# Turning the second half's input rows by VectorE ahead of time, by way of DRAM, instead of by TensorE amid the projections

## The chip, the cores and the metric

One core of a Trainium2 chip runs the whole step. The metric is device time in microseconds. Before the change the median of three runs is 1445.81 us (1445.39 to 1446.68).

## The reference

One layer of a hybrid decoder: prompt of 2048 tokens (`x_prompt`, 1024 wide) and 8 sample tokens, everything in float32.

```
ada = silu(c) @ w_ada + b_ada
shift, scale, gate = split(ada, 3)
hn = rmsnorm(x, g_norm) * (1 + scale) + shift
z = hn @ w_in                                    # 1024 -> 5136 columns
xa, za, q, k, v, glr, zg = split(z)
# LRU group: conv4 over xa, two block-diagonal gates, linear recurrence, times silu(za)
# GLA group: 4 heads, o = chunked linear attention of q, k, v with decay from glr,
#            o = rmsnorm(o) * g_gla_norm, times silu(zg)
x = x + gate * (concat(y_lru, y_gla) @ w_out)
y = rmsnorm(x, g_final)
```

The rows of `x` lie with tokens first; a projection on TensorE wants `hn` with its 1024 features on the partitions. So each block of 128 tokens has to be normalised, turned (128 tokens x 1024 features become 8 blocks of 128 features x 128 tokens), and modulated by scale and shift, which after the turn are values per partition (`Gm`, `Sh`).

## The kernel before, in words

The prompt is worked in two halves of 1024 tokens. The turned `hn` of the current half stays in SBUF as two tiles, `hh` (rounded to the matmul's type) and `hl` (what the rounding left), and a product of `hn` with a weight is three matmuls: high with high, low with high, high with low (L661 to L663 in `project`, L346 to L348 for values). Weights of `w_in` are split the same way by ScalarE and VectorE in the first half, stored to DRAM as `parts`, and loaded from there in the second (L293, `w<-parts`, 1 MB for a pair of high and low).

The program is written by a driver with a clock of its own (`tick`, `after`): `after(units, fn)` puts a piece of work in a heap, and it is written out when the clock has passed that time. A second list, `drips`, holds pieces that `project` writes out between its matmuls, one for every two steps of the contraction (every four for 256 columns). A scheduler then orders the instructions of each engine by its own model of time, so an engine's order is fixed when the program is built; each engine works its order through, and an instruction that waits holds up what stands behind it. `behind(V)` has it put an instruction directly after the last one on VectorE. SP's queue issues most of the DMAs, and is in order too.

Tiles come from pools with a fixed number of buffers: `xt` (tag "xt" in pool `xp`) has two, PSUM `acc` four, PSUM `tp` two. Whoever takes a buffer again waits until it was read.

The place of the change is the end of half 0, `lru_last_a`, in which the last LRU column tile (`xa_unit`, `za_unit`, gates L1315 to L1317) is projected for half 0 while `hh` and `hl` are overwritten, 256 tokens at a time, by the second half's:

- `hn_load(g)` for g = 0 to 3 loads two blocks of 128 rows of the second half (L256; into the two `xt` buffers for g = 0, into three `xst` tiles for g = 1 to 3), and `normalize` squares and sums them (ScalarE, L165), takes 1/sqrt by twelve small VectorE steps (L147 to L153) and scales (L181).
- `next_hn` calls `modulate`, dripped: eight transposes by TensorE for four of the eight feature blocks of a pair of row blocks (L197, into `tp`), an eviction with scale and bias by ScalarE (L199, L201; for g = 3 every second one by VectorE, L203), the high part by GpSimd (L204) and the low part by VectorE (L205).

After it comes `gates_ahead`: the gate columns of one head over the new half, as two products of 256 tokens, two more of 256 and two of 512 (evicted by L1129 and L1130, stored to `zgd`), the sums of quarter blocks of `hn` that a seven-product scheme needs (`sums`, L1491 to L1500 on VectorE, `drips` as well), and the products themselves (`seven`, L1559).

Of the kernel before, what the change touches and what calls it, by code (L numbers as in the profile page):

```python
# [8 lines left out]
F32 = mybir.dt.float32  # L9
F32R = mybir.dt.float32r  # L10
I32 = mybir.dt.int32
AF = mybir.ActivationFunctionType
OP = mybir.AluOpType

P = 128
D = 1024
KT = D // P
T = 2048
TH = T // 2
NS = 8  # L20
# [34 lines left out]
def hybrid_kernel(ctx, tc, i, o):  # L55
    nc = tc.nc
    V, S, G, PE, SP = nc.vector, nc.scalar, nc.gpsimd, nc.tensor, nc.sync

    const = ctx.enter_context(tc.tile_pool(name="const", bufs=1))
    dpool = ctx.enter_context(tc.tile_pool(name="dpool", bufs=1, space=bass.MemoryType.DRAM))  # L60
    psum = ctx.enter_context(tc.tile_pool(name="psum", bufs=1, space=bass.MemoryType.PSUM))

    def acc():
        return psum.tile([P, 512], F32, tag="acc", name="acc", bufs=4)

    def tps():
        return psum.tile([P, 512], F32, tag="tp", name="tp", bufs=2)
# [7 lines left out]
    wd2 = dpool.tile([2, P, 2, 4, 512], F32, tag="wd2", name="wd2")  # L75
    zd = dpool.tile([16, P, D], F32, tag="zd", name="zd")
    zgd = dpool.tile([8, P, TH + NS], F32, tag="zgd", name="zgd")
    a21d = dpool.tile([2, P, 4, 512], F32, tag="a21d", name="a21d")
    twd = dpool.tile([3 + len(EARLY), 4, P, 2, 512], F32, tag="twd", name="twd")

    ident = const.tile([P, P], F32, name="ident")
# [4 lines left out]
    xp = p1.enter_context(tc.tile_pool(name="xp", bufs=2))  # L86
# [24 lines left out]
    Gm = cp.tile([P, KT, 9], F32, name="Gm")  # L111
    Sh = cp.tile([P, KT, 9], F32, name="Sh")
# [29 lines left out]
    def rsqrt(pool, out, ss, n, rows, scale):  # L142

        y = pool.tile([P, 16], F32, tag="rs_y", name="rs_y", bufs=1)[:rows, :n]
        t = pool.tile([P, 16], F32, tag="rs_t", name="rs_t", bufs=1)[:rows, :n]
        x = pool.tile([P, 16], F32, tag="rs_x", name="rs_x", bufs=1)[:rows, :n]
        V.tensor_scalar(x, ss, scale, EPS, op0=OP.mult, op1=OP.add)  # L147
        V.tensor_scalar(t.bitcast(I32), x.bitcast(I32), 1, None, op0=OP.logical_shift_right)
        V.tensor_scalar(y.bitcast(I32), t.bitcast(I32), -1, 0x5F3759DF, op0=OP.mult, op1=OP.add)
        for it in range(3):  # L150
            V.tensor_tensor(t, y, y, op=OP.mult)
            V.scalar_tensor_tensor(t, t, -0.5, x, op0=OP.mult, op1=OP.mult)
            V.scalar_tensor_tensor(out if it == 2 else y, t, 1.5, y, op0=OP.add, op1=OP.mult)  # L153
# [9 lines left out]
    def square_sum(pool, out, x, m, n, tag="f512"):  # L163
        junk = pool.tile([P, 1024], mybir.dt.bfloat16, tag=tag, name="junk", bufs=2)
        S.activation(junk[:m, :n], x, AF.Square, accum_out=out)  # L165

    def squares(pool, xt, m=P, tag="f512", ss=None, j0=0):
        if ss is None:
            ss = pool.tile([P, 4], F32, tag="ss", name="ss", bufs=2)
        for j, x in enumerate(xt, j0):  # L170
            square_sum(pool, ss[:m, j:j + 1], x[:m], m, D, tag)
        return ss

    def scales(pool, ss, n, m=P):
        rs = pool.tile([P, 4], F32, tag="rs", name="rs", bufs=2)
        rsqrt(pool, rs[:m, :n], ss[:m, :n], n, m, 1.0 / D)
        return rs

    def times(xt, rs, m=P, j0=0):
        for j, x in enumerate(xt, j0):  # L180
            V.tensor_scalar(x[:m], x[:m], rs[:m, j:j + 1], None, op0=OP.mult)  # L181

    def normalize(pool, xt, m=P, tag="f512"):

        times(xt, scales(pool, squares(pool, xt, m, tag), len(xt), m), m)

    def modulate(xt, g, kts):

        c = slice(g * 256, (g + 1) * 256)
        for k2 in range(kts[0], kts[1], 2):  # L190
            pt = tps().rearrange("p (k t) -> p k t", k=2)
            cg = slice(g % 2 * 256, g % 2 * 256 + 256)
            f = (fs4[(1, 2, 0)[k2 // 4 if g < 2 else 2]][:, k2 % 4:k2 % 4 + 2, cg] if g < 2 or k2 >= 4
                 else ra[k2 // 2][:, :, cg])
            for kt in range(2):
                for j in range(2):
                    PE.transpose(pt[:, kt, j * P:(j + 1) * P],  # L197
                                 xt[j][:, (k2 + kt) * P:(k2 + kt + 1) * P], ident)
            S.activation(f[:, 0], pt[:, 0], AF.Identity, scale=Gm[:, k2, 8:9], bias=Sh[:, k2, 8:9])  # L199
            if g < 3:  # L200
                S.activation(f[:, 1], pt[:, 1], AF.Identity, scale=Gm[:, k2 + 1, 8:9], bias=Sh[:, k2 + 1, 8:9])  # L201
            else:
                V.tensor_scalar(f[:, 1], pt[:, 1], Gm[:, k2 + 1, 8:9], Sh[:, k2 + 1, 8:9], op0=OP.mult, op1=OP.add)  # L203
            G.tensor_scalar(hh[:, k2:k2 + 2, c], f, 1.0, 0.0, op0=OP.mult, op1=OP.add)  # L204
            V.tensor_tensor(hl[:, k2:k2 + 2, c], f, hh[:, k2:k2 + 2, c].bitcast(F32), op=OP.subtract)  # L205

# [35 lines left out]
            V.tensor_tensor(hl[:, kt, :256], f[:, j], hh[:, kt, :256].bitcast(F32), op=OP.subtract)  # L242
        split(1)

    def hn_load(g, now=True):

        xt = []
        for j in range(2):
            q = 2 * g + j
            if q < 2:  # L250
                x = xp.tile([P, TH + NS], F32, tag="xt", name="xt")[:, :D]
            else:
                n = q - 2
                x = xst[n // 2][:, n % 2]
            t0 = TH + q * P
            SP.dma_start(x, i["x_prompt"][0, t0:t0 + P])  # L256
            xt.append(x)
        if now:
            normalize(xp, xt)
        return xt  # L260

    fs = cp.tile([P, KT, NS], F32, name="fs")
# [174 lines left out]
    with tc.tile_pool(name="ada", bufs=1, side="right") as ap:  # L437
# [79 lines left out]
        with in_order():  # L517
# [13 lines left out]
            pt = turn(xt0[0:2], (0, 1))  # L531
# [10 lines left out]
            for c in range(1, 4):  # L542
                k = (2 * c, 2 * c + 1)
                if c > 1:
                    ada(c, (0, KT))
                pt = [turn(xt0, (kt,)) for kt in k]
# [134 lines left out]
    def behind(q):  # L681

        return tc.issue_after(next(x for x in reversed(list(nc.cur_bb.bb.instructions)) if x.engine == q.engine))
# [17 lines left out]
    def after(units, fn, gla=False, val=False):  # L701
        clock[1] += 1
        heapq.heappush(pend, (clock[0] + units, clock[1], fn, gla, val))
# [17 lines left out]
    def ada_gate():  # L721

        pg = acc()

        def step(kt):
            ws = [xp.tile([P, TH + NS], F32, tag="xt", name="xt")[:, :D] for _ in range(2)]
            for n, w in enumerate(ws):
                SP.dma_start(w, i["w_ada"][0, (kt + n) * P:(kt + n + 1) * P, 2 * D:])

            def mm():  # L730
                for n in (1, 0):
                    for g in range(4):
                        PE.matmul(pg[32 * g:32 * g + 32, :256], sc[:, kt + n], ws[n][:, g * 256:(g + 1) * 256],
                                  start=kt == 0 and n == 1, stop=kt == KT - 2 and n == 0)
                if kt + 2 < KT:
                    step(kt + 2)
                else:
                    gr = xp.tile([P, 512], F32, tag="f512", name="gr")[:, :256]
                    S.copy(gr, pg[:, :256])
                    SP.dma_start(gated, gr)  # L740
                    after(4, lambda: ready("gate"))
            after(3, mm)

        step(0)


    so, fs4, xst, ra, waiting = {}, [], [], [], ["gate", "pairs"]
    outw = {"stop": False, "next": None, "busy": False}

    def ready(what):  # L750
        nonlocal hp
        waiting.remove(what)
        if what == "pairs":
            hpx.close()
            hp = hpx.enter_context(tc.tile_pool(name="hp", bufs=1, reuse_waits="tile"))
        if not waiting:
            out_weights()
# [670 lines left out]
    def next_hn(xt, g, k):  # L1428

        modulate(xt[g], g, (k, k + 4))  # L1430
        if (g, k) == (1, 0):
            normalize(xp, xt[3])

    def lru_last_a(js):

        xa_load, xa_unit, za_load, za_unit = lru_units(0)
        xt = [hn_load(0)]
        lru(0, js[:-2])
        outw["stop"] = True
        lru(0, js[-2:-1])  # L1440
        t = xa_load(js[-1])
        za_load(t)
        flush_gla()
        while outw["busy"]:
            heapq.heappop(pend)[2]()
        open_sp()
        xt += [hn_load(1), hn_load(2), hn_load(3, False)]
        for s in range(2):
            xa_unit(t, s)
            za_unit(t, s)  # L1450
            for g in range(2 * s, 2 * s + 2):
                for k in range(0, KT, 4):
                    drips.extend([lambda g=g, k=k: next_hn(xt, g, k), lambda: None])
# [503 lines left out]
    for x in pairs[:2]:  # L1957
        x.new(A11)
        r = wp.tile([P, 1088], F32, tag="wr", name="wr")[:, :D].rearrange("p (q k t) -> p q k t", q=2, k=4)
# [215 lines left out]
    for n in range(2, 16):  # L2175
        g = n - 1
        x, prev = pairs[n], pairs[n - 1]
# [16 lines left out]
    for q in range(8):  # L2194
        g, k = 2 + q // 2, q % 2
# [63 lines left out]
```

## Time and profile before

| what | before |
|---|---|
| median of 3 runs | 1445.81 us |
| the profiled execution | 1445.69 us |
| its span | 1443.8 us, so 1.9 us lie outside the span |
| mean granted TensorE clock | 0.998 |
| busy share PE, DVE, ACT, POOL | 98%, 73%, 48%, 15% |
| HBM | 188.51 MB read, 115.33 MB written, 210 GB/s over the span |
| TensorE transposes of L197 | 64, from 558.7 to 588.0 us |

PE is TensorE, DVE VectorE, ACT ScalarE, POOL GpSimd, SP SyncE; PEld are TensorE's weight loads, and a q behind an engine's name its queue. A row of a timeline has the start, the duration, the engine, the line, the operation, what it writes and reads, and in brackets the idle time before it with what ended it. A row of groups has the count, the busy time, the mean of one in ns, and the idle time before it. Half 0's projections fill about 80 to 560 us, the turn of the second half's rows 547 to 590, the products of the second half follow from there.

### The profile page before, as it was taken

Reading aid. Unit: us, or ns where it says so; the run is one execution under the profiler, and the core shown is the slowest. Engines: PE = TensorE matmul, PEld = TensorE weight load, DVE = VectorE, ACT = ScalarE, POOL = GpSimd, SP = SyncE. Lnnn points to the kernel's source line nnn. Section 1 sums busy time; section 2 is a strip of 40 time slices with the busy share of each in tenths; the row PEclk is TensorE's granted clock in tenths of the full one; section 3 lists DMA queues with packets and bytes.
Section 4 is the critical chain, followed back from the end, with each engine's and each line's share of the span. In section 5 each row is a group of like instructions: output and inputs, shape, how many; then the busy total and the mean of one; then the engine's idle time right before and its main releaser. Section 6 shows DMA issues by size and latency. Waiting matters only on the chain.

```text
span 1443.8 us, 23568 instructions
## 1 busy us (share of the span) xinstructions
PE 1421.8 (98%) x8741; PEld 1250.8 (87%) x8741; DVE 1050.4 (73%) x2473; ACT 689.4 (48%) x1251; POOL 220.5 (15%) x366
## 2 busy tenths in 40 slices
PE   8999999999999999999999999999999999999998
PEld 6889979899898988878899999999998887778886
DVE  5767658776676678955458688686888986688886
ACT  3654444663445358624354454635557622144342
POOL 0200112122112013100111422334210000000000
PEclk9999999999999999999999999999999999999999
DMA  9755785874565546577744665665671767694453
GB/s 321 278 186 176 251 274 191 259 244 148 192 218 189 182 162 228 177 245 236 286 148 151 210 237 178 225 198 182 238 254 66 293 231 267 227 353 144 134 166 117
DMA packets 160856, 305.33 MB, mean 211 GB/s; under 512 B 12962, under 2 KB 90434, under 8 KB 158301
## 3 DMA queue, kind: packets, MB, share of 16 engines
q1 hardware_dynamic: 106837, 217.39, 44.1%
q0 software_dynamic: 22912, 70.96, 14.4%
q10 hardware_dynamic: 30992, 15.47, 3.6%
q8 instruction: 69, 1.13, 0.3%
q14 instruction: 46, 0.38, 0.1%
HBM read 188.51 MB, written 115.33 MB: 210 GB/s over the span
## 4 chain that ended last, share of the span: by engine, by line
PE 79%; DVE 9%; ACT 4%; issue 3%; DMA 3%; SPq 1%; POOL 0%; ACTq 0%; DVEq 0%; POOLq 0%
PE acc L1845 12%; PE acc L661 11%; PE acc L663 11%; PE acc L662 11%; PE tp L1845 9%; PE acc L1559 6%; PE acc L346 3%; PE acc L347 3%; PE acc L348 3%; PE po L1072 2%; PE acc L1315 1%; PE tp L1163 1%; PE acc L1317 1%; PE acc L1316 1%; PE tp L1041 1%
## 5 line engine op out<-in xcount | busy, mean ns | idle before, releaser
L661 PE MATMUL acc<-hh,w 128*128 128x512 f32 (+3 forms) x1112 | 377.4, 339 | 0.3 <-ACT tx L1318 0.2
L663 PE MATMUL acc<-hh,w 128*128 128x512 f32 (+3 forms) x1112 | 375.1, 337 | 0.0
L662 PE MATMUL acc<-hl,w 128*128 128x512 f32 (+3 forms) x1112 | 375.0, 337 | 0.0
L661 PEld LDWEIGHTS acc<-hh,w 128*128 128x128 f32 x1112 | 209.3, 188 | 16.8 <-ACT tx L1318 0.9
L663 PEld LDWEIGHTS acc<-hh,w 128*128 128x128 f32 x1112 | 209.2, 188 | 16.1
L662 PEld LDWEIGHTS acc<-hl,w 128*128 128x128 f32 x1112 | 209.3, 188 | 15.1
L1845 PE MATMUL acc<-w,a 128*128 128x512 f32 (+1 forms) x792 | 184.9, 387 | 0.0
L1845 PEld LDWEIGHTS acc<-w,a 128*128 128x128 f32 x792 | 146.8, 188 | 33.2 <-issue 3.4
L346 PE MATMUL acc<-w,hh 128*128 128x256 f32 (+1 forms) x508 | 143.9, 283 | 0.0
L348 PE MATMUL acc<-w,hl 128*128 128x256 f32 (+1 forms) x508 | 142.8, 281 | 0.1
L347 PE MATMUL acc<-w,hh 128*128 128x256 f32 (+1 forms) x508 | 142.7, 281 | 0.0
L1845 PE MATMUL tp<-w,a 128*128 128x512 f32 x564 | 136.1, 391 | 0.0
L1845 PEld LDWEIGHTS tp<-w,a 128*128 128x128 f32 x564 | 105.2, 188 | 26.9 <-issue 5.2
L346 PEld LDWEIGHTS acc<-w,hh 128*128 128x128 f32 x508 | 95.6, 188 | 1.3 <-ACT zs L1129 0.4
L348 PEld LDWEIGHTS acc<-w,hl 128*128 128x128 f32 x508 | 96.1, 189 | 0.3 <-DVE hl L228 0.3
L347 PEld LDWEIGHTS acc<-w,hh 128*128 128x128 f32 x508 | 95.5, 188 | 0.2
L1129 ACT ACTIVATE zs<-acc 128x512 f32<-128x512 f32 (+3 forms) x70 | 34.4, 492 | 107.8 <-PE acc L663 102.8
L1695 ACT CAST a<-s 128x512 fp32r<-128x512 f32 x61 | 36.5, 620 | 95.0 <-issue 35.5
L1278 DVE SCALAR_TENSOR_TENSOR cv<-xa,vecT,cv 128x512 f32<-128x512 f32 (+2 forms) x120 | 76.6, 641 | 3.1 <-ACT cv L1276 2.7
L1130 DVE SCALAR_TENSOR_TENSOR zs<-zs,acc 128x512 f32<-128x512 f32 (+3 forms) x70 | 38.4, 548 | 46.8 <-ACT zs L1129 46.8
L956 ACT CAST vh<-acc 128x256 fp32r<-128x256 f32 x56 | 20.4, 370 | 86.2 <-PE acc L348 70.8
L957 DVE TENSOR_TENSOR vl<-acc,vh 128x256 fp32r<-128x256 f32 x56 | 23.2, 419 | 47.6 <-ACT vh L956 47.6
(409 smaller groups left out, 2757.5 us busy)
## 6 DMA issues: line engine op xcount, KB each, us to landing
parts<-w SPq DMA_DIRECT2D x37, 1024.0 KB
w<-parts SPq DMA_DIRECT2D x28, 1024.0 KB
wr<-in_w_in_dram SPq DMA_DIRECT2D x38, 512.0 KB
a<-mixd SPq DMA_DIRECT2D x63, 256.0 KB
w<-wd SPq DMA_DIRECT2D x12, 1024.0 KB
w<-twd SPq DMA_DIRECT2D x20, 512.0 KB
wada<-in_w_ada_dram SPq DMA_DIRECT2D x16, 512.0 KB
mixd<-zs ACTq DMA_DIRECT2D x32, 256.0 KB
```

The lines of the kernel that those rows point to most:

```text
L346: PE.matmul(ps, hh[:, kt, c], hi[:, kt % 4], start=kt == 0, stop=False)
L347: PE.matmul(ps, hh[:, kt, c], lo[:, kt % 4], start=False, stop=False)
L348: PE.matmul(ps, hl[:, kt, c], hi[:, kt % 4], start=False, stop=kt == KT - 1)
L661: PE.matmul(ps[:, :n], hi[:, kt], a, start=kt == 0, stop=False)
L662: PE.matmul(ps[:, :n], hi[:, kt], b, start=False, stop=False)
L663: PE.matmul(ps[:, :n], lo[:, kt], a, start=False, stop=kt == KT - 1)
L1129: S.activation(z, ps, AF.Tanh, scale=0.5)
L1130: V.scalar_tensor_tensor(z, z, 1.0, ps, op0=OP.add, op1=OP.mult)
L1278: V.scalar_tensor_tensor(cv[:, cq], xa[:, cq.start + k:cq.stop + k], cw[k], cv[:, cq], op0=OP.mult, op1=OP.add)
L1559: PE.matmul(ps, w[:, u, k], x[v][k], start=start and (k, u, v) == (0, 0, 0), stop=(k, u) == (3, 1), skip_group_check=True)
L1695: S.copy(t[:, 0, k], (low(t) if src is None else src)[:, k])
L1845: PE.matmul(ps, t[:, u, k], w[:, v, k, c], start=(q < 3 or ps is own) and (k, u, v) == (0, 0, 0), stop=(k, u) == (3, 1), skip_group_check= ...
```

## The change

The second half's eight blocks of rows are no longer turned by TensorE. From the end of `ada_gate` on, early in half 0, a chain written by `after` handles one block q after another: load the rows (an `xt` buffer), three clock units later square and sum them, then the small steps and the scaling, then a VectorE transpose of all 32x32 blocks of the 128x1024 tile into the other `xt` buffer, then a store to a new DRAM tile `xtd[q]`, then the next block. VectorE turns each 32x32 block in place within its group of 32 partitions. What is left of the turn, the exchange of partition groups and column groups, is done by the addresses of the loads: `hn_load` reads `xtd` with four DMAs for each tile, one for each group of 32 partitions, in pieces of 1 KB (twenty loads where there were eight). `modulate` then reads the turned tiles in SBUF: no PSUM, and for g = 0 twice as many, half as wide ScalarE instructions, since the two blocks lie in two tiles.

```diff
+    xtd = dpool.tile([8, P, D], F32, tag="xtd", name="xtd")
...
     def modulate(xt, g, kts):
...
+        pt = [x.rearrange("p (n k t) -> p k n t", k=KT, t=32) for x in xt]
         for k2 in range(kts[0], kts[1], 2):
-            pt = tps().rearrange("p (k t) -> p k t", k=2)
...
-            for kt in range(2):
-                for j in range(2):
-                    PE.transpose(pt[:, kt, j * P:(j + 1) * P],
-                                 xt[j][:, (k2 + kt) * P:(k2 + kt + 1) * P], ident)
-            S.activation(f[:, 0], pt[:, 0], AF.Identity, scale=Gm[:, k2, 8:9], bias=Sh[:, k2, 8:9])
-            if g < 3:
-                S.activation(f[:, 1], pt[:, 1], AF.Identity, scale=Gm[:, k2 + 1, 8:9], bias=Sh[:, k2 + 1, 8:9])
-            else:
-                V.tensor_scalar(f[:, 1], pt[:, 1], Gm[:, k2 + 1, 8:9], Sh[:, k2 + 1, 8:9], op0=OP.mult, op1=OP.add)
+            for kt in range(k2, k2 + 2):
+                for j, y in enumerate(pt):
+                    n = 256 // len(pt)
+                    z = f[:, kt - k2, j * n:(j + 1) * n].rearrange("p (n t) -> p n t", t=32)
+                    if g < 3 or kt == k2:
+                        S.activation(z, y[:, kt], AF.Identity, scale=Gm[:, kt, 8:9], bias=Sh[:, kt, 8:9])
+                    else:
+                        V.tensor_scalar(z, y[:, kt], Gm[:, kt, 8:9], Sh[:, kt, 8:9], op0=OP.mult, op1=OP.add)
             G.tensor_scalar(hh[:, k2:k2 + 2, c], f, 1.0, 0.0, op0=OP.mult, op1=OP.add)
...
+    def turn_ahead(q):
+
+        x, w = [xp.tile([P, TH + NS], F32, tag="xt", name="xt")[:, :D] for _ in range(2)]
+        SP.dma_start(x, i["x_prompt"][0, TH + q * P:TH + (q + 1) * P])
+
+        def scaled(ss):
+            with behind(V):
+                times([x], scales(xp, ss, 1))
+            after(0.5, turned)
+
+        def turned():
+            with behind(V):
+                V.transpose(w.rearrange("p (c k j) -> p c k j", c=4, k=KT), x.rearrange("p (k c j) -> p c k j", c=4, k=KT))
+            after(0.5, stored)
+
+        def stored():
+            SP.dma_start(xtd[q], w)
+            if q < 7:
+                after(1, lambda: turn_ahead(q + 1))
+
+        def squared():
+            ss = squares(xp, [x])
+            after(0.5, lambda: scaled(ss))
+
+        after(3, squared)
+
+    def hn_load(g):
+
+        if g == 0:
+            xt = [xp.tile([P, TH + NS], F32, tag="xt", name="xt")[:, :D] for _ in range(2)]
+        else:
+            xt = [xst[g - 1].rearrange("p q d -> p (q d)")]
+        m = 2 // len(xt)
+        for j, x in enumerate(xt):
+            src = xtd[2 * g + j * m:2 * g + j * m + m].rearrange("q (a r) (c f) -> c r (q a) f", a=4, c=4)
+            for c in range(4):
+                SP.dma_start(x[32 * c:32 * c + 32].rearrange("r (n f) -> r n f", f=256), src[c])
         return xt
...
     def next_hn(xt, g, k):
 
         modulate(xt[g], g, (k, k + 4))
-        if (g, k) == (1, 0):
-            normalize(xp, xt[3])
```

In `ada_gate` the last line of the last step is now `turn_ahead(0)`, and `lru_last_a` still calls the four `hn_load`, the first before the last LRU tiles and three after `open_sp`.

Three places in the order of instructions. Line numbers of the changed kernel lie 22 or 23 higher from `hn_load` on (L293 is L315, L1130 is L1153, L1541 is L1562, L1491, L1495 and L1500 are L1512, L1516 and L1521).

SP's queue at the end of half 0, before: `w_6119` and `w_6121` are the weights of the first and second 256-wide product, `wg` gate weights.

```order
L293 DMA w_6119<-parts_1198 128x2x1024
L1367 DMA wg_6553<-parts_1512 128x512
L256 DMA xst_5825<-in_x_prompt_dram 128x1024 x2
L256 DMA xst_5826<-in_x_prompt_dram 128x1024 x2
L256 DMA xst_5827<-in_x_prompt_dram 128x1024 x2
L293 DMA w_6121<-parts_1205 128x2x1024
L1541 DMA w_6393<-parts_2391 128x2x512
```

The same place now: `w_6208` and `w_6210` are these weights, `xt_5477` is the second tile of g = 0, and `xst_6009` to `xst_6011` are g = 1 to 3; `xt_5370` is the eighth block, turned.

```order
L315 DMA w_6208<-parts_1199 128x2x1024
L1390 DMA wg_6602<-parts_1513 128x512
L281 DMA xst_6009<-xtd_70 32x8x256 x3
L281 DMA xt_5477<-xtd_70 32x4x256 x4
L281 DMA xst_6009<-xtd_70 32x8x256
L281 DMA xst_6010<-xtd_70 32x8x256 x2
L261 DMA xtd_70<-xt_5370 128x1024
L281 DMA xst_6010<-xtd_70 32x8x256 x2
L281 DMA xst_6011<-xtd_70 32x8x256 x4
L315 DMA w_6210<-parts_1206 128x2x1024
L1668 DMA zgd_69<-zs_6245 128x256
```

The weights of the second 256-wide product now stand behind the last loads of turned rows and behind the store of the eighth block.

VectorE at the same stage, before: the `zs` rows are evictions of 256-wide products, L203 and L205 make `hh` and `hl` of the last two blocks, and L1491 to L1500 are the sums.

```order
L1130 SCALAR_TENSOR_TENSOR zs_6213<-zs_6213,acc_6170 128x256
L205 TENSOR_TENSOR hl_128<-fs4_5823,hh_127 128x2x256
L203 TENSOR_SCALAR ra_5829<-tp_6230,Gm_107,Sh_108 128x256
L203 TENSOR_SCALAR ra_5830<-tp_6239,Gm_107,Sh_108 128x256
L205 TENSOR_TENSOR hl_128<-ra_5829,hh_127 128x2x256
L205 TENSOR_TENSOR hl_128<-ra_5830,hh_127 128x2x256
L1130 SCALAR_TENSOR_TENSOR zs_6260<-zs_6260,acc_6217 128x256
L203 TENSOR_SCALAR fs4_5823<-tp_6277,Gm_107,Sh_108 128x256
L203 TENSOR_SCALAR fs4_5823<-tp_6286,Gm_107,Sh_108 128x256
L205 TENSOR_TENSOR hl_128<-fs4_5823,hh_127 128x2x256 x2
L1130 SCALAR_TENSOR_TENSOR zs_6307<-zs_6307,acc_6264 128x256
L1330 SCALAR_TENSOR_TENSOR tx_6105<-tx_6105,cv_5887 128x1024
```

The same now: `zs_6282` is the eviction of the second 256-wide product, `zs_6319` that of the third, which frees the PSUM buffer of the first 512-wide one.

```order
L205 TENSOR_TENSOR hl_129<-ra_6013,hh_128 128x2x256
L205 TENSOR_TENSOR hl_129<-ra_6014,hh_128 128x2x256
L205 TENSOR_TENSOR hl_129<-fs4_6007,hh_128 128x2x256 x2
L1521 TENSOR_TENSOR fs4_6007<-fs4_6007,ra_6013 128x1024
L1521 TENSOR_TENSOR fs4_6007<-fs4_6007,ra_6014 128x1024
L1512 TENSOR_TENSOR ra_6013<-fs4_6008,ra_6013 128x1024
L1516 TENSOR_TENSOR so_6473<-fs4_6007,so_6472 128x1024
L1153 SCALAR_TENSOR_TENSOR zs_6282<-zs_6282,acc_6249 128x256
L1512 TENSOR_TENSOR fs4_6008<-fs4_6007,fs4_6008 128x1024
L1512 TENSOR_TENSOR ra_6014<-fs4_6008,ra_6014 128x1024
L1516 TENSOR_TENSOR so_6473<-fs4_6007,so_6472 128x1024
L1153 SCALAR_TENSOR_TENSOR zs_6319<-zs_6319,acc_6286 128x256
```

The evictions that stood among the last subtractions of L205 now stand behind four and seven of the sums.

VectorE early in half 0, at the first turned block (`on` is an attention output being scaled for its own transposes on TensorE; L1112 is L1089 before).

```order
L1153 SCALAR_TENSOR_TENSOR zq_2607<-zq_2607,acc_2580 128x8
L154 SCALAR_TENSOR_TENSOR ors_2512<-rs_t_2514,rs_y_2513 128x4
L257 STREAM_TRANSPOSE xt_2291<-xt_2290 128x1024
L1112 TENSOR_SCALAR on_2310<-on_2310,ors_2512 128x256 x4
L805 TENSOR_TENSOR tr_2276<-tr_2276,th_2612 128x512
```

The block transpose is new; the rows around it were there, and the scaling of `on` now comes behind it.

More of the change, by code (lines that the diff above doesn't have):

```diff
@@ L243, in apply_first @@
         split(1)
[L245 to L259, printed above, removed]
+    def turn_ahead(q):
[27 more added lines that the diff above has]
+                SP.dma_start(x[32 * c:32 * c + 32].rearrange("r (n f) -> r n f", f=256), src[c])
         return xt
@@ L741, in mm @@
                     after(4, lambda: ready("gate"))
+                    turn_ahead(0)
             after(3, mm)
@@ L1446, in lru_last_a @@
         open_sp()
-        xt += [hn_load(1), hn_load(2), hn_load(3, False)]
+        xt += [hn_load(1), hn_load(2), hn_load(3)]
         for s in range(2):
```

## The prediction

> **What bounds the kernel now.** I read the page first, then the busy times by stretch, then the lines that the change touches.
>
> ```profile
> PE 1421.8 (98%) x8741; PEld 1250.8 (87%) x8741; DVE 1050.4 (73%) x2473; ACT 689.4 (48%) x1251; POOL 220.5 (15%) x366
> PE 79%; DVE 9%; ACT 4%; issue 3%; DMA 3%; SPq 1%; POOL 0%; ACTq 0%; DVEq 0%; POOLq 0%
> 80.00:550.00 470.00, 468.73 (x2841) 414.64 (x2840) 323.80 (x730) 229.85 (x395) 79.90 (x136) 1.00 0.62 207
> 560.00:590.00 30.00, 29.40 (x202) 26.31 (x201) 28.84 (x70) 22.12 (x47) 10.96 (x14) 1.00 0.27 90
> 600.00:625.00 25.00, 23.00 (x98) 17.88 (x97) 22.35 (x24) 10.62 (x15) 2.60 (x4) 1.00 0.70 242
> ```
>
> The columns of the last three rows are the stretch and its length, then busy time of PE, weight loads, DVE, ACT and POOL, the granted clock, the DMA share and GB/s. TensorE is the bound: a microsecond of its queue is a microsecond of the kernel, and a microsecond of another engine costs only where TensorE waits for it. In the first half (80 to 550) PE is busy 468.7 of 470 us, with DVE idle for 146. In the stage that the change empties (560 to 590) DVE is as full as PE, 28.8 of 30 us. From 600 to 625 PE loses 2 us.
>
> The transposes are the lines of L197:
>
> ```profile
> L197 PE MATMUL tp<-ident,xst x48: 270/272/328, 566.1 to 588.0; 128*128 128x128 f32 x48
> L197 PE MATMUL tp<-ident,xt x16: 270/272/330, 558.7 to 564.8; 128*128 128x128 f32 x16
> PE tp L197 <- DVE xst L181: 0.6, 2, 0.3
> 558.42 0.40 PE L663 MATMUL acc<-hh,w 128*128 128x512 f32 x1
> 558.66 1.03 PE L197 MATMUL tp<-ident,xt 128*128 128x128 f32 x8
> 559.45 0.48 PE L661 MATMUL acc<-hh,w 128*128 128x512 f32 x1
> 559.76 0.39 PE L662 MATMUL acc<-hl,w 128*128 128x512 f32 x1
> 559.99 0.40 PE L663 MATMUL acc<-hh,w 128*128 128x512 f32 x1
> 573.35 0.28 PE L661 MATMUL acc<-hh,w 128*128 128x256 f32 x1
> 573.46 0.28 PE L662 MATMUL acc<-hl,w 128*128 128x256 f32 x1
> 590.90 0.39 PE L661 MATMUL acc<-hh,w 128*128 128x512 f32 x1
> ```
>
> The 270 ns of one transpose is its latency, not its price, since they overlap. Without transposes matmuls start 0.23 us apart when 512 wide (559.76 to 559.99) and 0.12 when 256 wide (573.35 to 573.46). From 558.42 to 559.76 two steps take 1.34 us instead of 0.46: a batch of eight costs 0.88.
>
> **The change part by part.** *TensorE, removed.* Between 558.42 and 573.35 PE runs 49 matmuls 512 wide, 11.15 us at their pace; the stretch takes 14.93, so 3.8 us go. From 573.35 to 590.90 there are 96 of 256 wide and 6 gate products of 512, 12.9 us of 17.55: 4.65 go. Together 8.4 us, 0.6 of it the wait on DVE. If nothing else were late, the first 512-wide product with the second columns would move from 590.90 to 582.5.
>
> *The early part, eight turned tiles amid half 0.* Per tile VectorE now does twelve small steps, a scaling and a block transpose, ScalarE a square, SP a load and a store.
>
> ```profile
> L165 ACT ACTIVATE junk<-xst 128x1024 bf16<-128x1024 f32 x6 | 6.4, 1080 | 1.9 <-DMA xst<-in_x_prompt_dram 1.8
> 562.27 0.16 DVE L152 SCALAR_TENSOR_TENSOR rs_t<-rs_t,rs_x 128x2 f32<-128x2 f32 x1
> L181 DVE TENSOR_SCALAR xst<-xst,rs 128x1024 f32<-128x1024 f32 x6 | 4.6, 807 | 0.0
> L1491 DVE TENSOR_TENSOR fs<-fs,fs 128x1024 f32<-128x1024 f32 x4 | 4.8, 1208 | 0.0
> L1334 DVE TENSOR_TENSOR_SCAN tg<-xl,tx 128x1024 f32<-128x1024 f32 x2 | 4.6, 2280 | 0.0
> 225.65 1.13 DVE L1089 TENSOR_SCALAR on<-on,ors 128x256 f32<-128x256 f32 x4
> 226.13 1.13 PE L1163 MATMUL tp<-ident,on 128*128 128x128 f32 x8
> ```
>
> The trace has no block transpose. A pass over 128x1024 costs 0.8 us with one operand (L181), 1.2 with two (L1491), 2.3 as a scan (L1334). I take 1.2, and 0.8 and 2.3 as bounds. [...] A tile is then 12 x 0.2 + 0.8 + 1.2 = 4.4 us of DVE, 35 us for eight (two of the eight were scaled in this stretch before), in 146 us of idle DVE time, and 8 x 1.1 = 9 us of ScalarE in 240 idle. Both stand in the queue ahead of things that PE waits for in one place only: the first block transpose stands right before the scaling of `on` at 225.65, and PE follows that by 0.5 us at 226.13 (L1163). The filler around it moves forward by some 0.5, so PE stalls about 0.6 there. SP's loads and stores are cheap beside a DMA share of 0.62; the weight loads behind each waiting store are wanted a projection later, some 5 us. I take +0.6 for this part, bounds 0 and +3.5 (another 1.2-us transpose in front of PE two or three times).
>
> *VectorE and ScalarE in the last stage, removed.* Six scalings (4.6 us), three chains of twelve small steps and six squares (6.4) go; ScalarE now reads SBUF. This relieves DVE and would also end the stall from 600 to 625, whose sums come late on DVE:
>
> ```profile
> 609.95 4.49 PE L1559 MATMUL acc<-so,w 128*128 128x512 f32 x19
> 617.68 0.47 PE L1559 MATMUL acc<-hh,w 128*128 128x512 f32 x1 [1.17 <-DVE hl L1495]
> 618.83 0.50 PE L1559 MATMUL acc<-ra,w 128*128 128x512 f32 x1 [0.45 <-DVE ra L1495]
> 623.88 0.39 PE L1559 MATMUL acc<-hl,w 128*128 128x512 f32 x1
> ```
>
> 48 products from 609.95 take 10.9 us at their pace and here end at 623.88: 3.0 us of stall.
>
> *What the last stage gains as waits.* The eighth tile's block transpose writes a buffer that the first two turned tiles, read back, also pass through. In the new order it therefore stands behind ScalarE's eight readings of the second of these tiles. Behind it on SP: its store, two loads, the four loads of the last tile pair (they need the store), and only then the 1 MB of weights for the second 256-wide product, which was issued at 564.45 before. TensorE waits for those weights.
>
> ```profile
> 561.93 0.62 ACT L1295 CAST xh<-cv 128x512 fp32r<-128x512 f32 x1 [0.23 <-issue]
> 566.06 0.62 ACT L1394 COPY xa<-acc 128x512 f32<-128x512 f32 x1
> L854 ACT CAST p<-r 128x256 fp32r<-128x256 f32 x1 | 0.4, 407 | 0.8 <-DVE r L850 0.8
> 547.00 4.02 SPq L256 DMA_DIRECT2D xst<-in_x_prompt_dram  x6
> 564.45 0.56 SPq L293 DMA_DIRECT2D w<-parts  x1
> 572.18 0.52 SPq L1541 DMA_DIRECT2D w<-parts  x1
> 584.42 1.87 SPq L1647 DMA_DIRECT2D zgd<-zs  x2
> 586.26 0.38 ACT L1129 ACTIVATE zs<-acc 128x256 f32<-128x256 f32 x1 [1.13 <-DMA zgd<-zs]
> out_dram<-xt POOLq DMA_DIRECT2D x4, 512.0 KB, 4.7
> GB/s 407 292 134 216 148 270 268 410 421 412 426 423 404 325 95 173 0 131 412 161 0 0 138 212 0 0 0 11 0 0 87 87 0 378 397 412 397 163 22 333
> ```
>
> The last row is the DMA rate from 540 to 600 in slices of 1.5 us. The 1 MB issued at 564.45 moves in slices 18 to 20 and ends near 569.1: 4.7 us. The 512 KB issued at 572.18 moves in slices 23 and 24 and ends near 575.3: 3.1 us. A 128 KB store issued at 584.42 lets ScalarE go at 586.26: 1.8. One issue is 4.02/6 = 0.67 us.
>
> The clock of the new chain: the copy at 566.06 stood behind eight evictions of 0.45 us; without them the copy and the conv step follow the cast of 561.93 and are done near 564.1. Eight 128x128 readings, at 0.28 each (a 128x256 one from SBUF took 0.41), end at 566.3. DVE finishes what it is at and transposes, until about 569.1. The store takes 3.3 us (between 1.8 for 128 KB and 4.7 for 512 KB from POOL; nearest the 3.1 of a 512 KB load): 572.5. Four issues: 575.1. Then two paths part:
> - Weights issued by 575.5, landed by 580.2. PE reaches this product at 572.5 (569.6, that is 573.35 less 3.8, plus 24 x 0.12) and stalls 7.7 us; after it 3 x 2.88 us of 256-wide products and 1.4 of gates: ready for the 512-wide one at 590.2.
> - The last pair lands at 577.4 (2.3 after its last issue, between 1.8 and 3.1). ScalarE 0.4, four POOL conversions of 0.9 and the last subtraction give 582.4. DVE's order then has four sum steps, an eviction, three sum steps and the eviction that frees the PSUM buffer of the first 512-wide product:
>
> ```profile
> L204 POOL TENSOR_SCALAR hh<-fs 128x512 fp32r<-128x512 f32 x12 | 9.7, 819 | 21.6 <-ACT fs L201 18.9 <-DVE fs L203 2.1 <-POOL hh L204 0.3
> L205 DVE TENSOR_TENSOR hl<-fs,hh 128x512 fp32r<-128x512 f32 x12 | 8.9, 749 | 0.4 <-POOL hh L204 0.4
> L1130 DVE SCALAR_TENSOR_TENSOR zs<-zs,acc 128x256 f32<-128x256 f32 x4 | 1.6, 406 | 0.0
> ```
>
> Seven of those sums lie in front (two of L1521, three of L1512, two of L1516), at 1.14 apart, and two evictions of 0.4: 8.8 us, that is 591.2. Before, these evictions stood between the subtractions.
>
> The later end decides: the 512-wide product starts at 591.2 instead of 590.9. The 8.4 us are spent on the wait for weights and evictions. What stays is the later stall: the sums have now begun before the products that need them, so the 3.0 us go.
>
> **Sum**, against the profiled 1445.69: -8.4 + 8.7 - 3.0 + 0.6 = -2.1, so 1443.6. The profiled run is 0.12 below the median of 1445.81, which changes nothing.
>
> **The rivals.** *Full gain.* If the eighth transpose, or the weight load behind it, comes early enough that PE never waits, -8.4 stays and the sums move with it: 1445.7 - 8.4 + 0.6 = 1437.9. For it: only the last of eight tiles is held, by a buffer alone. Against: the new SP order puts store, loads and weights in one line, and PE reaches the weights at 572.5, earlier than the store can land. Chance 0.13.
>
> *The round trip is dearer, and it is slower.* Each microsecond on the way from the eighth transpose to the landing of the last pair is a microsecond of PE. With a transpose of 2.3 instead of 1.2, a store of 4.7 instead of 3.3, readings by ScalarE at the 0.45 of evictions (+1.4) and pieces of 1 KB that land in 4.7 instead of 2.3, the product starts at 597.5: 6.3 more, 1449.9. Zero is at 2.1 us more, that is 593.3, and slower by over 0.2% needs 596.2. For it: nothing on the path is shown in the trace. Chance 0.22. [...]
>
> *VectorE is the wrong place.* The transposes stand in front of what PE needs in half 0 as at 226, not once but at four of the eight, 1.2 each: 0.6 + 4.8 more, 1448.4. For it: DVE is busy 324 of 470 us there, in bursts, and the order on each engine is fixed when the program is built. Against: PE waited for hardly anything in that stretch. Chance 0.15. [...]
>
> **How the numbers follow.** Forecast 0.50, with a range of its own from 1441.0 to 1446.2 (both paths 2 us earlier or later, early part 0 to 1.2); full gain 0.13; dear round trip 0.22; VectorE 0.15. 0.2% (2.9 us) is about what a measurement of this kernel can tell from no change. Faster by that, below 1442.8: 0.13 and two fifths of the forecast, 0.33. Slower, above 1448.6: 0.17 of the round trip, 0.09 of VectorE, and 0.04 of a forecast whose bounds add up: 0.30. Same: 0.37. The range, 1437.9 to 1451.0, reaches to the full gain and a little past the dear trip.
>
> **What would show it right or wrong.** Right: PE runs from 569.6 without transposes, then waits some 7 us on a weight load before the second 256-wide product, and the 512-wide one starts near 591; no waits on sums between 600 and 625; the block transpose lasts about 1.2 us; the eighth comes after 566. Wrong: PE without a wait at 572 (full gain), a 512-wide start after 596, or PE behind block transposes in half 0.

## The result, and the profile after

The change takes 1451.74 us (median of 6 runs, 1450.14 to 1453.35) against 1445.82: a ratio of 1.0041 (95% interval 1.0028 to 1.0054). It is slower by some 6 us, where 1443.6 was forecast and the range ended at 1451.0. The profiled execution took 1451.16 us, its span is 1449.4, and its mean granted clock 0.993 instead of 0.998. The page and the stretches of the kernel after:

```profile
PE 1412.9 (97%) x8677; PEld 1244.8 (86%) x8677; DVE 1064.7 (73%) x2529; ACT 693.2 (48%) x1259; POOL 221.1 (15%) x366
PE 82%; DVE 6%; issue 4%; ACT 4%; DMA 3%; POOL 1%; SPq 0%; DVEq 0%; ACTq 0%; POOLq 0%
80.00:550.00 470.00, 466.53 (x2829) 412.36 (x2827) 345.13 (x818) 234.94 (x405) 79.88 (x136) 1.00 0.66 220
560.00:590.00 30.00, 17.54 (x90) 15.46 (x89) 23.69 (x36) 17.93 (x37) 12.82 (x16) 0.80 0.78 220
590.00:600.00 10.00, 10.00 (x68) 9.59 (x68) 10.00 (x11) 4.72 (x7) 0.00 (x0) 0.90 0.36 135
600.00:625.00 25.00, 25.00 (x112) 20.68 (x111) 18.35 (x20) 14.92 (x18) 2.12 (x3) 1.00 0.71 235
```

TensorE's busy time fell by 8.9 us, and the time still rose. The place is the second row of stretches: of 30 us PE is busy for 17.5, and the granted clock is 0.80. From 600 to 625 the stall of before is gone. What TensorE waited for, 80 to 800 us, and its timeline around it:

```profile
PE acc L683 <- DVE fs L203: 12.5, 1, 12.5
PE acc L683 <- DVE vl L980: 1.4, 1, 1.4
PE acc L368 <- DVE rs_y L150: 0.8, 1, 0.8
573.72 0.28 PE L685 MATMUL acc<-hh,w 128*128 128x256 f32 x1
586.45 0.55 PE L683 MATMUL acc<-hh,w 128*128 128x256 f32 x1 [12.46 <-DVE fs L203]
586.80 0.41 PE L684 MATMUL acc<-hl,w 128*128 128x256 f32 x1
587.02 0.41 PE L685 MATMUL acc<-hh,w 128*128 128x256 f32 x1
592.06 0.28 PE L685 MATMUL acc<-hh,w 128*128 128x256 f32 x1
598.96 0.39 PE L683 MATMUL acc<-hh,w 128*128 128x512 f32 x1
```

The second 256-wide product waits 12.5 us, and the first 512-wide one starts at 598.96 instead of 590.90. The wait is put down to L203, which ended just before; but this product does not read what L203 makes. By the order it waits for its weights. SP's queue with two of its waits (for the eighth block's transpose, then for its store to land), then the DMA rate from 570 to 590 in slices of 0.5 us, then the rates of two stretches of that time:

```profile
548.44 2.72 SPq L281 DMA_DIRECT2D xst<-xtd  x3
558.51 1.73 SPq L281 DMA_DIRECT2D xt<-xtd  x4
560.28 5.95 SPq L281 DMA_DIRECT2D xst<-xtd  x3
572.54 0.34 SPq L261 DMA_DIRECT2D xtd<-xt  x1
572.93 4.47 SPq L281 DMA_DIRECT2D xst<-xtd  x6
577.50 0.56 SPq L315 DMA_DIRECT2D w<-parts  x1
SPq L261 <- DVE xt L257: 6.2, 1, 6.2
SPq L281 <- DMA xtd<-xt: 1.3, 1, 1.3
GB/s 0 0 0 0 0 0 115 401 393 164 285 201 254 229 123 119 264 211 205 193 209 221 203 197 205 217 270 360 410 410 408 377 412 418 176 385 410 422 406 401
576.00:582.00 6.00, 0.00 (x0) 0.00 (x0) 3.00 (x6) 3.82 (x9) 1.81 (x3) 0.69 1.03 202
582.50:586.00 3.50, 0.00 (x0) 0.00 (x0) 3.27 (x6) 1.76 (x4) 1.80 (x4) 0.50 1.02 350
```

The store of the eighth block moves at 400 GB/s (573.5 to 574.5). The six loads behind it, 1.5 MB in loads of 32 partitions each, move at 202 GB/s with all DMA engines busy (share 1.03), until about 583. Only then comes the 1 MB of weights, at 410 GB/s, to about 586.3: 8.8 us after its issue, where 4.7 was reckoned. The last columns show a second loss: the granted clock falls to 0.69 and 0.50 while PE waits.

```profile
L257 DVE STREAM_TRANSPOSE xt<-xt x8: 1231/1236/1245, 225.1 to 571.3; 128x1024 f32<-128x1024 f32 x8
584.24 1.09 ACT L201 ACTIVATE ra<-xst,Sh,Gm 128x256 f32<-128x256 f32 x2 [1.75 <-DMA xst<-xtd]
594.05 0.41 DVE L1153 SCALAR_TENSOR_TENSOR zs<-zs,acc 128x256 f32<-128x256 f32 x1
597.79 0.41 DVE L1153 SCALAR_TENSOR_TENSOR zs<-zs,acc 128x256 f32<-128x256 f32 x1
```

The block transpose takes 1.24 us, the eighth at 571.3. The last pair lands at 584.2 instead of the forecast 577.4, and the eviction that frees the buffer of the 512-wide product ends at 598.2. That is the second path of the forecast, 7.0 us later than reckoned. It ends 0.8 us before the product starts, and TensorE has no gap from 586.45 on, so the path of the weights decided, not this one as forecast.

I matched TensorE's matmuls of the two traces in their order. Against before, the changed kernel is 1.3 us early at 40 us, 1.3 early at 180 and at 279, 1.3 late at 310, 1.4 late at 540, 8.1 late at the first 512-wide product, 5.1 from 621 on, where the sums' stall of before is over, and 5.5 at the end. So half 0 costs 2.7, the last stage 6.6, and the sums give 3.0 back. The early start is not the change's: the traces of the twelve kernels below lie between 1.1 early and 0.2 late at 40 us, whatever was done to them.

### The profile page after: what moved, and what is told of

The parts are those of the page before. It is cut to its first block, busy times and chain, and to the rows that moved or that the text cites. A ratio compares the mean times of both kernels' runs of the same rounds, so it can differ in the third digit from the quotient of the medians.

```text
span 1449.4 us, 23539 instructions
## 1 busy us (share of the span) xinstructions
PE 1412.9 (97%) x8677; PEld 1244.8 (86%) x8677; DVE 1064.7 (73%) x2529; ACT 693.2 (48%) x1259; POOL 221.1 (15%) x366
## 4 chain that ended last, share of the span: by engine, by line
PE 82%; DVE 6%; issue 4%; ACT 4%; DMA 3%; POOL 1%; SPq 0%; DVEq 0%; ACTq 0%; POOLq 0%
PE acc L1866 12%; PE acc L683 11%; PE acc L685 11%; PE acc L684 11%; PE tp L1866 9%; PE acc L1580 6%; PE acc L368 3%; PE acc L369 3%; PE acc L370 3%; PE po L1095 2%; PE acc L1338 1%; PE tp L1064 1%; DMA twd<-th 1%; PE acc L1340 1%; PE acc L1339 1%
## 5 line engine op out<-in xcount | busy, mean ns | idle before, releaser
L683 PE MATMUL acc<-hh,w 128*128 128x512 f32 (+3 forms) x1112 | 378.1, 340 | 14.1 <-DVE fs L203 12.5
L1153 DVE SCALAR_TENSOR_TENSOR zs<-zs,acc 128x512 f32<-128x512 f32 (+3 forms) x70 | 38.4, 549 | 42.0 <-ACT zs L1152 42.0
```

Of the source, the lines that this page charges most:

```text
L683: PE.matmul(ps[:, :n], hi[:, kt], a, start=kt == 0, stop=False)
L1153: V.scalar_tensor_tensor(z, z, 1.0, ps, op0=OP.add, op1=OP.mult)
```

## The experiments

**Two by two: the held block, and the form of the loads.** In the first kernel the first pair of turned blocks is loaded after `open_sp`, so that the eighth transpose has a buffer. In the second the exchange of partition groups is moved from the loads to the stores: a load is then one 128-partition DMA of 4 KB rows.

```diff
-        xt = [hn_load(0)]
...
-        xt += [hn_load(1), hn_load(2), hn_load(3)]
+        xt = [hn_load(g) for g in range(4)]
```

```diff
-            SP.dma_start(xtd[q], w)
+            dst = xtd[q].rearrange("(c r) (a f) -> a r c f", c=4, a=4)
+            for a in range(4):
+                SP.dma_start(dst[a], w[32 * a:32 * a + 32].rearrange("r (c f) -> r c f", c=4))
...
-            for c in range(4):
-                SP.dma_start(x[32 * c:32 * c + 32].rearrange("r (n f) -> r n f", f=256), src[c])
+        for j in range(2):
+            x = xt[j] if g == 0 else xst[g - 1][:, j]
+            SP.dma_start(x, xtd[2 * g + j])
```

> The first pair of turned blocks is loaded after the last tile's weights are under way, so that the eighth block transpose no longer waits for a buffer; nothing else is changed (pieces of 1 KB stay). Theory A (the loss is the wait for the weights of the second 256-wide product, queued behind loads of turned rows that the held eighth block delayed): the loads are all issued from 548 on, the weights by 565, no wait of TensorE near 574, time 1438 to 1441 us. Rival B (the evictions of the 256-wide products stand behind the sums on VectorE and hold the first 512-wide product): a wait of 4 to 8 us moves to that product, 1443 to 1447. Rival C (the loss is in half 0, where VectorE's transposes stand in front of what TensorE needs): stays at 1449 to 1452.

> The 1 KB pieces move from the loads to the stores of the turned blocks (four stores of 32 partitions each per block, then one load of 4 KB rows per block: 8 loads instead of 20); the eighth block is still held. Theory A with the slow pieces as its main part (loads in 1 KB pieces move at 205 GB/s, and the weights stand behind them): loads at about 400 GB/s, TensorE waits 3 us or less near 574, the last pair is still late (its second block lands near 580), time 1441 to 1446. If the hold of the eighth block is the main part and the pieces are not: 1448 to 1451. Rival C: 1449 to 1452.

> Both: no hold of the eighth block, and 4 KB pieces in the loads. Theory A: no wait of TensorE over 1 us between 565 and 600, the first 512-wide product starts at 583 to 585, time 1437 to 1440 us. Rival B: a wait at the first 512-wide product, 1443. Rival C: 1449 or more.

| | eighth block held | not held |
|---|---|---|
| loads of 32 partitions, 1 KB pieces | 1451.7 (the change) | 1450.6, ratio 1.0032 (1.0019 to 1.0044) |
| loads of 128 partitions, 4 KB rows | 1441.6, 0.9966 (0.9953 to 0.9978) | 1436.9, 0.9937 (0.9924 to 0.9949) |

The form of the loads is worth 10 us with the hold and 14 without; the hold 1 us with slow loads and 5 with fast. These are prices of whole edits, since with the moved stores the order of instructions changed in two more places. In the second kernel SP issues the weights ahead of the held store, at 562.87 and 568.50:

```profile
562.87 0.55 SPq L315 DMA_DIRECT2D w<-parts  x1
568.50 1.77 SPq L263 DMA_DIRECT2D xtd<-xt  x4
```

And around the third block of half 0 VectorE's order differs: by matched matmuls half 0 costs 1.0 and 0.8 us in the two kernels with moved stores, against 2.7 and 3.0 in the two without, so some 2 of the 10 and 14 us lie there.

My expectation of the first kernel missed: its SP queue with that queue's longest wait, its rate and TensorE's waits show why.

```profile
550.21 21.71 SPq L281 DMA_DIRECT2D xst<-xtd  x12
572.02 0.56 SPq L315 DMA_DIRECT2D w<-parts  x1
SPq L281 <- DMA mixd<-zs: 8.8, 2, 8.5
552.00:571.00 19.00, 19.00 (x86) 15.73 (x85) 15.29 (x19) 17.42 (x33) 6.22 (x6) 1.00 1.04 236
PE acc L683 <- DMA w<-parts: 3.1, 1, 3.1
PE acc L683 <- DVE zs L1153: 2.8, 1, 2.8
PE acc L1338 <- DVE zs L1153: 2.1, 1, 2.1
```

The eighth block holds nothing now, and issuing twelve loads still takes 21.7 us. SP waits 4.5 us for earlier loads of turned rows and 8.8 us for a store of ScalarE's queue, `mixd<-zs`. In the trace each of these loads waits until the DMA that last used its semaphore has landed. The two queues share eight semaphores (101 and 104 to 110 in the records of the change), so a longer row of loads meets its own forerunners and such a store. The weights leave at 572.0. The rest of the wait goes to the evictions behind the sums. With both mended, the weights leave at 563.59, and the 512-wide product starts at 583.10, where the forecast had it without waits (582.5). Its six loads are issued in 4 us without such a wait:

```profile
547.65 3.98 SPq L281 DMA_DIRECT2D xst<-xtd  x6
563.59 0.56 SPq L315 DMA_DIRECT2D w<-parts  x1
550.00:557.00 7.00, 7.00 (x32) 5.80 (x31) 4.07 (x5) 6.40 (x12) 0.62 (x1) 1.00 1.02 399
560.00:590.00 30.00, 30.00 (x179) 26.82 (x178) 29.93 (x44) 23.76 (x45) 13.25 (x14) 1.00 0.50 174
583.10 0.39 PE L683 MATMUL acc<-hh,w 128*128 128x512 f32 x1
```

This kernel beats both, at 1436.91 us (1436.2 to 1438.47).

**What in the form of the loads.** Three kernels complete the picture: the mended kernel with each load cut into four of 32 partitions, the first kernel with loads that reach 128 partitions in pieces of 1 KB, and the latter with the hold.

```diff
-            SP.dma_start(x, xtd[2 * g + j])
+            for c in range(0, P, 32):
+                SP.dma_start(x[c:c + 32], xtd[2 * g + j, c:c + 32])
```

```diff
+            src = xtd[2 * g + j].rearrange("(a r) (c f) -> a c r f", a=4, c=4)
+            for b in range(4):
+                SP.dma_start(x[:, 256 * b:256 * b + 256], src[b])
```

> As the kernel with both mended (4 KB rows, eighth block not held, 1436.9), with each 512 KB load cut into four of 32 partitions. If the 32 partitions are the cause: about 200 to 230 GB/s from 548 on, the last lands after 566, TensorE waits 5 us or more in the last stage, 1445 to 1451. If the pieces are: 1437 to 1438.

> As the kernel whose first pair is loaded late (eighth block not held, 1450.6 with loads of 32 partitions), with loads of 128 partitions and 1 KB pieces; SP's order is otherwise the same. If the 32 partitions are the cause: time within 3 us of the kernel with both mended (1436.9), so 1437 to 1440. If the pieces are: 1448 to 1451.

> The change with each block loaded by four loads that all reach 128 partitions (one for each group of 32 rows of the store, pieces of 1 KB as in the change) instead of four of 32 partitions; the eighth block is still held. The weights of the second 256-wide product come ahead of the held store in SP's order by that. If the 32 partitions of a load make the loads slow: rate 270 GB/s or more, no wait of over 3 us near 574, time 1441 to 1444, close to the kernel with 4 KB rows (1441.6). If the 1 KB pieces do: near 205 GB/s, waits of 5 us or more, 1447 to 1452.

Loads of 32 partitions with 4 KB rows: 1448.7 us, ratio 1.0015 (1.0006 to 1.0024), so 11.8 us of the mended kernel's gain are lost again, with 22.3 us for 24 issues and a wait for the weights. Not all of that is the rate, as SP's queue shows:

```profile
SPq L282 <- DMA mixd<-zs: 6.7, 1, 6.7
```

For 6.7 us SP waits for the store `mixd<-zs`, and from 559 to 560 the DMA engines move nothing. So this kernel does not part the 32 partitions from the number of loads, 24 instead of 6. Nor do the 1.9 us by which the first kernel is slower (1450.6) price the pieces of 1 KB: the stores differ too, and half 0 costs 1.7 us here and 3.0 there. The two kernels with 128 partitions and 1 KB pieces missed both expectations: 1463.7 (ratio 1.0120, 1.0107 to 1.0134) and 1467.0 (1.0145, 1.0131 to 1.0158). The stretch of the former:

```profile
548.43 36.41 SPq L281 DMA_DIRECT2D xst<-xtd  x24
555.00:574.00 19.00, 14.77 (x66) 11.89 (x64) 9.05 (x11) 6.23 (x13) 2.59 (x2) 0.96 0.27 91
```

The DMA engines are busy for a share of 0.27 (other DMAs included), at 91 GB/s, where the first kernel has 1.04 and 236 GB/s. The outermost dimension of these addresses is the four column groups; whether that holds the engines back is not shown. The pieces alone do not: loads of 128 partitions in 1 KB pieces reach a share of 0.97 and 318 GB/s in the kernel cut by columns below. These two kernels therefore say nothing on the 1 KB pieces.

**The form alone, in the kernel before.** The six loads of 512 KB at 547 us are cut: by columns into four (128 partitions, 1 KB), by rows into four (32 partitions, 4 KB), by rows into two (64 partitions, 4 KB).

```diff
-            SP.dma_start(x, i["x_prompt"][0, t0:t0 + P])
+            for c in range(0, P, 32):
+                SP.dma_start(x[c:c + 32], i["x_prompt"][0, t0 + c:t0 + c + 32])
```

> The kernel before, whose six loads of second-half blocks at 547 us are each cut into four loads of 256 columns: all 128 partitions, pieces of 1 KB instead of 4 KB, same data. If the piece sets the rate: about 205 GB/s while these 3 MB move instead of about 410, so the last lands some 7 us later; the loads are early enough that the time hardly moves, 1446 to 1449. If the rate belongs to the 32 partitions of a load: 410 GB/s stays.

> The kernel before, whose six loads at 547 us are each cut into four loads of 32 rows: 32 partitions each, pieces of 4 KB as before. If the piece sets the rate: about 400 GB/s as before, time 1445 to 1447. If the 32 partitions of a load set it: about 205 GB/s, and 1446 to 1449.

> The kernel before, whose six loads at 547 us are each cut into two loads of 64 rows (partitions 0 to 63 and 64 to 127, rows of 4 KB). Loads of 32 partitions moved at 233 GB/s and made that kernel 1455.0 us, loads of 128 at 419. If the rate grows with the number of partitions: 64 of them give 300 GB/s or more and 1445 to 1448 us. [...]

Stretches while the loads move, for the kernel before, by columns and 32 partitions, and for 64 partitions the DMA rate from 546 in slices of 0.5 us; its first two blocks are still whole loads.

```profile
551.00:558.00 7.00, 7.00 (x33) 5.79 (x32) 5.74 (x5) 5.07 (x9) 0.00 (x0) 1.00 1.03 419
552.00:558.00 6.00, 6.00 (x30) 4.97 (x29) 6.00 (x9) 3.75 (x6) 0.00 (x0) 1.00 0.97 318
553.00:557.00 4.00, 4.00 (x20) 3.30 (x19) 4.00 (x4) 1.19 (x2) 0.00 (x0) 1.00 1.03 233
GB/s 25 197 336 262 279 246 328 385 393 406 442 426 381 270 262 205 246 238 229 229 238 246 221 246 238 229 246 221 246 238 229 238 246 213 233 240 371 345 264 224
```

By columns: 318 GB/s, neither of the two rates expected, and 1446.2 us, the same (1.0005, 0.9996 to 1.0014). 32 partitions: 233 GB/s, near the 205 expected of them, and 1455.0 us (1.0065, 1.0051 to 1.0079), which is more than expected. TensorE waits 8.9 us for its transposes: the form of the loads costs 9 us with nothing turned ahead. Both kernels have 24 loads, so the number of loads does not set the rate; but of the 9 us, too, a part may be SP's queue, which waits 5.1 us for `mixd<-zs` here and not by columns. 64 partitions move at 205 to 246 GB/s from 553.5 on, no faster than 32, where the whole blocks ahead of them moved at up to 442. So the rate did not grow with the partitions from 32 to 64, and missed the 300 GB/s or more expected of that; why it did not is not shown. The time did not follow as far: 1447.7 (1.0008, 0.9998 to 1.0018), with 12 loads issued in 13.9 us instead of 24 in 20.9.

**Half 0 alone.** The kernel before with blocks 0 to 6 turned ahead for nothing: the last stage loads, normalises and transposes as before.

```diff
+                    turn_ahead(0)
...
+            if q < 6:
+                after(1, lambda: turn_ahead(q + 1))
```

> The kernel before, with the turning ahead of blocks 0 to 6 added in half 0 and its result not used: the last stage loads, normalises and transposes as before, so that some work is done twice (no eighth block, which would be held there). What half 0 pays for loads, squares, scalings, block transposes and stores shows alone. If half 0 costs what the trace of the change showed between 200 and 560 us: 1 to 3 us, time 1447 to 1449. If half 0 is free: 1446. Rival C (the loss is mostly in half 0): 1450 or more.

1448.55 us, ratio 1.0018 (1.0009 to 1.0027): 1.3 to 3.9 us. By matched matmuls nothing is lost until 279 us, and 2.6 from there to 310, where the third block's small steps and its transpose stand ahead of what TensorE waits for. It is the place of the 2.7 in the change itself. The waits of half 0:

```profile
PE acc L688 <- DVE vl L985: 1.1, 1, 1.1
PE acc L373 <- DVE rs_y L150: 0.9, 1, 0.9
```

**The weights alone.** One kernel writes the last pair's loads after the weights, the other issues these weights by POOL. In both the scheduler also put the first step of the last 512-wide gate product ahead, and this product's values are not the reference's; the amount of work is.

```diff
-        xt += [hn_load(1), hn_load(2), hn_load(3)]
+        xt += [hn_load(1), hn_load(2)]
+        turned4.append(xt)
...
         w = [weights(ZG + (2 * h + dt) * P, P) for dt in range(2)]
+        turned4[0].append(hn_load(3))
```

```diff
-            SP.dma_start(both[:, :, c].bitcast(F32), parts[col, k0])
+            (G if col == ZG + (2 * HEADS[0] + 1) * P else SP).dma_start(both[:, :, c].bitcast(F32), parts[col, k0])
```

> The loads of the last pair of turned blocks are written after the weights of the gate columns, so that SP issues the 1 MB of weights ahead of these four loads; hold and 1 KB pieces stay. Theory A: the weights land 4 to 6 us earlier, TensorE waits 6 to 8 us instead of 12.5 near 574, the last pair lands a little later, time 1445 to 1448. Rival B (evictions behind sums decide, whenever the weights come): no gain beyond 1 us, 1450 to 1452. Rival C: same as the change, 1451.

> The change, with the 1 MB of weights of the second 256-wide product issued by POOL's queue instead of SP's, ahead of the loads that they stood behind. If that wait is the whole loss of the last stage: TensorE runs on at 574, the first 512-wide product near 585, time 1439 to 1441. If the late landing of the last pair and the evictions behind the sums come next (theory of two waits, one behind the other): TensorE runs on at 574 and waits 6 to 12 us for its 512-wide product, which starts at 592 to 597; time 1444 to 1449. If the load shares the slow transfers: a wait near 574 stays, 1450.

1455.57 us (ratio 1.0060, 1.0046 to 1.0074) and 1459.86 (1.0100, 1.0087 to 1.0114). The waits of the first, then of the second:

```profile
PE acc L683 <- DVE hl L205: 7.5, 1, 7.5
PE acc L683 <- POOL hh L204: 3.3, 1, 3.3
```

```profile
PE acc L683 <- POOL hh L204: 17.1, 1, 17.1
```

With the weights 2.7 us earlier the first wait shrinks from 12.5 to 7.5; with POOL's queue TensorE runs on past 574 and through its gates at 583.85. So the wait near 574 is one for the weights. But then TensorE waits for the last pair, longer than the gain. In the second kernel this is not the loads' doing, as a stretch of that wait and ScalarE's first reading of the last pair show:

```profile
588.00:600.00 12.00, 0.00 (x0) 0.00 (x0) 8.09 (x9) 10.71 (x17) 3.10 (x4) 0.54 0.00 0
594.75 1.08 ACT L201 ACTIVATE ra<-xst,Sh,Gm 128x256 f32<-128x256 f32 x2
```

The DMA moves nothing, so the pair has landed. ScalarE reads it late, behind gate work that comes after these readings in the change. My expectations of the time missed for that reason: the order on ScalarE and TensorE changed too, and what the weights alone cost is not shown by these two.

## Why the prediction was wrong

- **What the last stage gains as waits** is the step that failed, in the size of the loads. The place was right: SP's line of store, loads and weights, and a wait before the second 256-wide product, forecast at 7.7 us and measured at 12.5. The transpose (1.24 us for 1.2) and the store (landed 3.1 us after its issue, for 3.3) were right, though the transposed tile was ready at 572.5 instead of 569.1: the stage began 1.4 late, ScalarE's eight readings took 3.2 us for 2.2, and three subtractions stood ahead on VectorE. But "landed by 580.2" and "landed at 577.4" took landing times from loads of 128 partitions, where these reach 32: 202 GB/s, the weights at 586.3 and the pair at 584.2. The weights needed 8.8 us from their issue where 4.7 was reckoned, which is 4.1 of the 4.8 us by which the wait exceeded the forecast. That the 32 partitions set the rate is shown by the cut loads of the kernel before (233 GB/s, against 318 for as many loads of 128 partitions and 419 for whole ones); the times of those kernels have SP's waits in them as well.
- **A term was missing.** After the 12.5 us wait the 26 steps from 586.45 to 592.06 take 5.6 us instead of 3.1, at a granted clock of 0.50: 2.5 us. The forecast's own 7.7 us wait should have had such a term: after the wait of 7.5 us with the weights first, the clock came back only after 3.6 us.
- **The sum of the last stage:** -8.4 + 12.5 + 2.5 = 6.6, as matched. The forecast had -8.4 + 8.7 = 0.3. That TensorE loses 8.4 us of transposes held; in the mended kernel it runs from 560 to 590 without a gap.
- **The early part** was 0.6 with bounds 0 to 3.5. Measured in place: 2.7, all of it at the third block, between 279 and 310. The stall foreseen at 226 did not show.
- **The sums' stall** of 3.0 went as forecast: 3.0 by matched matmuls.
- **The rivals.** "The round trip is dearer" (1449.9) is nearest, and its chance was 0.22; it had the pieces of 1 KB as one of four small causes, and not the partitions. Of the other three, the transpose and the store came out as the forecast had them, and the readings by ScalarE came 0.40 us apart, near the rival's 0.45. "VectorE is the wrong place" holds for 2 of the 8 us. "Full gain" was what the design can do: 1437.9 forecast, 1436.9 measured once loads and hold are mended. That the two lie so close is partly luck: the kernel is 7.8 us early at the first 512-wide product, as that rival had it, then gains 2.3 at the sums, which the rival left out, and loses 1.4 later.
- **In sum:** the profiled execution is 7.6 above the forecast: 6.3 of the last stage (6.6 for 0.3) and 2.1 of half 0 (2.7 for 0.6), less 1.3 by which it started early. A rest of 0.5 arises after 700 us; its cause was not sought.

## What to carry to other kernels

Price a DMA by what it reaches, not by its bytes: a transfer that a layout forces into groups of 32 partitions ran at half rate here (202 and 233 GB/s against 399 and 419), and what stood behind it on the queue paid: the weights took 8.8 us from their issue where 4.7 was reckoned. Count the DMAs too: 24 loads of 32 partitions in place of 6 whole ones made SP wait for another queue's store (6.7 and 5.1 us), and twelve made it wait for its own loads as well (4.5 us). If an exchange of partition groups must go through DRAM, put the odd form on the side that nobody waits for, here the stores early in half 0, and let the load be one of all partitions. A wait on TensorE cost more than itself here, since TensorE came back at half clock (0.50): 2.5 us more after the wait of 12.5.

## What the runs showed of the hardware

The clock in the stretch after the wait, then in the next one:

```profile
587.00:588.00 1.00, 1.00 (x7) 1.00 (x6) 1.00 (x2) 0.00 (x0) 0.84 (x1) 0.50 0.74 281
592.00:593.00 1.00, 1.00 (x10) 1.00 (x10) 1.00 (x2) 1.00 (x2) 0.00 (x0) 1.00 0.66 254
```

After the 12.5 us wait the clock stays at 0.50 for 5.5 us of full work; it had fallen at 578.3, 4.3 us into the wait. The time to the return varies: 3.6 us after the wait of 3.1 in the first kernel of the two by two and after the 7.5 with the weights first, 6.9 after the 17.1. Loads of 32 partitions moved at 202 (1 KB) and 233 GB/s (4 KB), of 64 at 205 to 246, of 128 at 399 to 419 in 4 KB rows and 318 in 1 KB pieces, all with the DMA engines busy (shares 0.97 to 1.06). In the cut kernel 24 loads of 32 partitions took 20.9 us to issue, with the DMA idle for moments at 558 us: there SP waits 5.1 us for the store `mixd<-zs` of ScalarE's queue, which the trace shows on the semaphore of the load that waits. No run kept the 24 loads and took that wait away.
